# A decoder layer with 32 experts on one core: experts' weights in 1 MB units with 8 KB rows, shift and scale as columns, logits normalized late

## The chip, the core and the metric

The kernel is one launch on one core of a Trainium2 chip. The metric is device time in microseconds (us). TensorE multiplies, VectorE (DVE) and ScalarE (ACT) work on rows of 128 partitions, GpSimd (POOL) does some element work and issues a few DMAs, and SyncE (SP) issues nearly all DMAs, in order. Three runs of the kernel before took 1286.1, 1295.19 and 1295.77 us, with the median at 1295.19.

## The reference

One layer, 256 tokens of width 1024 (`h`), float32. A token mixer (three attention branches, gates, output projection) is followed by a norm, an adaLN modulation by a conditioning vector `c`, a top-4-of-32 mixture of experts with clamped SwiGLU, and a last norm:

```python
x = layer_norm(DN_ALPHA * x + (1.0 + gate) * y, ln1_g, ln1_b)      # y: the mixer's output
shift, scale, gate = split(silu(c) @ mod_ffn_w + mod_ffn_b, 3)
h = x * (1.0 + scale) + shift
logits = h @ router_w + router_b
top_v, top_i = top_k(logits, 4);  combine = one_hot(top_i) * softmax(top_v)
for e in range(32):
    gu = h @ w_gu[e] + b_gu[e]                  # 1024 x 2048
    gate = minimum(gu[:, 0::2], 7.0); up = clip(gu[:, 1::2], -7.0, 7.0)
    act = (up + 1.0) * (gate * sigmoid(1.702 * gate))
    out += combine[:, e:e+1] * (act @ w_down[e] + b_down[e])       # 1024 x 1024
x = layer_norm(DN_ALPHA * x + (1.0 + gate_ffn) * out, ln2_g, ln2_b)
```

Each expert has 12.58 MB of weights, and all 32 have 402.65 MB. Every one is read once.

## The kernel before

**Stages.** By the trace: input projections to about 60 us, keys and values to 100, attention in 24 steps to 222, the branches' products and the output projection to 267, norm and router to 288, the sweep over the experts to 1258, the last norm to 1285.

**Experts.** The experts are sorted by how many tokens chose them, and each is worked on at a *place* with a fixed number of slots: 128 (`Wide`), 64 (`Narrow`) or 32 (`Few`). Four narrow experts come first (0 to 3); then cycles of narrow, wide, few, few. An expert takes 24 steps `t` of half a unit of weights. For a group of places `Group.choose` builds one-hot matrices `sel` on POOL, `Group.gather` brings the tokens' columns into `X` by matmuls with `sel`, `Group.slots` turns `sel` into `selT`, and `Group.weights` gathers the combine weights into `wsl`. Weights are the moving operand of fp32 matmuls (`raw,X` for gate and up, `raw,an` for down; the trace counts two instructions for each fp32 matmul, in two passes). Narrow and few experts split the array in column tiles: a narrow one runs two matmuls side by side, a few one four, so their rows in `y` stand at partitions 0 to 63 and 64 to 127 (or in quarters). A narrow and a few expert are both called split here; there are 25 of them, and 7 wide ones.

**Scatter.** `weigh` (L1288 to L1292) turns an expert's output `y` into two float32r tiles: `yh` on ScalarE, scaled by `wsl`, and the remainder `yl` on VectorE. `leave` then adds both into the four PSUM banks `acc` with `selT` as weights: eight one-pass matmuls, for split experts in pairs of row tiles (`tile_position=(64 n, 0)`), to different banks.

**Loads.** `Stream` hands out weights. `add_units` cuts a unit of 1 MB in two halves, `slot` gives each half a buffer of 512 KB (37 of them, in turn), and one DMA (L148) of 128 rows of 4 KB brings it. In the stages ahead of the experts a unit is one DMA of 1 MB with 8 KB rows, split by `high` (ScalarE) and `low` (VectorE, L165) into `hi` and `lo` tiles of 1024 columns, up to three halves ahead of their use. SP issues in order, a DMA waits for its buffer.

**Conditioning.** `mod_row` makes one row of 1024 of the modulation: `begin` loads a start value into `acc` by an SP DMA, eight `half` tasks multiply and add on VectorE (L687), and `total` sums the partitions by a matmul with ones, two tasks after the last half. There are four rows: gate of layer 2 (`gate2_done`, which sends it to `g2d` by a POOL DMA), gate 1 (`g1h_done`), scale and shift of the experts' norm. `row` (L700) loads two rows to all partitions for the last two.

**Norm and router.** `add` makes the residual `x1` (two operations on VectorE for each of four parts), `spread` its mean and variance, `norm` the normalized `xr` (ScalarE). `turn_norm` transposes it, `logits` multiplies it by `rwg`, `turn_logits` transposes the logits back for the top four. `modulate` makes the experts' input `h2`, two operations of 128x1024 for each half of the tokens. `choose` builds the first group's `sel` on VectorE, and `sort_1` (from L1526) begins the sort of the experts.

TensorE, SP and POOL run in the order of the program; in norm and router VectorE and ScalarE do as well.

Of the kernel before, what the change touches and what calls it, by code (L numbers as in the profile page):

```python
# [16 lines left out]
S = 256  # L17
# [12 lines left out]
RAW_BUFS = 10  # L30
LOW_BUFS = 4
RAW_MORE = 11
PAIRS = 4
AHEAD = 4
# [49 lines left out]
class Stream:  # L84

    def __init__(self, nc, pool, ahead):
        self.nc, self.pool, self.ahead = nc, pool, ahead
        self.todo, self.highs, self.lows, self.parts, self.at = [], 0, 0, {}, {}  # L90
        self.extra, self.big, self.count, self.turn = None, None, 0, True

    def unit(self, ap, m=None):

        n = ap.shape[-1]
        m = m or n // 2
        t = self.pool.tile([128, 2048], F32, tag="raw", name="raw", bufs=RAW_BUFS // 2)
        self.nc.sync.dma_start(out=t[:, :n], in_=ap)
        return t[:, :m], t[:, m:n]

    def slot(self, lasting=False):


        total = RAW_BUFS + 4 + LOW_BUFS + RAW_MORE + 2 * PAIRS if self.turn else RAW_BUFS
        n = self.count % total
        if lasting and (n < RAW_BUFS or n >= total - 2 * PAIRS):
            self.count += RAW_BUFS - n if n < RAW_BUFS else total - n + RAW_BUFS
            n = RAW_BUFS
        self.count += 1
        if n < RAW_BUFS:  # L110
            if n % 2 == 0:
                self.pair = self.pool.tile([128, 2048], F32, tag="raw", name="raw", bufs=RAW_BUFS // 2)
            return self.pair[:, n % 2 * 1024:n % 2 * 1024 + 1024]
        n -= RAW_BUFS
        for pool, tag, bufs in ((self.pool, "hi", 4), (self.pool, "lo", LOW_BUFS), (self.extra, "raw2", RAW_MORE)):
            if n < bufs:
                return pool.tile([128, 1024], F32, tag=tag, name="raw", bufs=bufs)
            n -= bufs
        if n % 2 == 0:
            self.pair = self.big([128, 2048], "raw")  # L120
        return self.pair[:, n % 2 * 1024:n % 2 * 1024 + 1024]

    def low_slot(self):
        return self.pool.tile([128, 1024], F32R, tag="lo", name="lo", bufs=LOW_BUFS)

    def rounded(self):
        return self.pool.tile([128, 1024], F32R, tag="hi", name="hi", bufs=4)

    def add(self, key, get, n=2048, whole=()):

        self.at[key] = len(self.todo)
        self.todo.append((key, get, n, whole))

    def high(self, last):

        while self.highs <= min(last, 2 * len(self.todo) - 1):
            half = self.highs
            u, s = divmod(half, 2)
            key, get, n, whole = self.todo[u]
            m = n // 2  # L140
            if s == 0:
                self.cur = get()
                if not isinstance(self.cur, tuple):
                    self.cur = self.unit(self.cur)
            src = self.cur[s]
            if s in whole:
                src = self.slot()
                self.nc.sync.dma_start(out=src, in_=self.cur[s])  # L148
            self.parts[half] = [src, None, None, m]
            self.highs += 1  # L150
            if s in whole:
                continue
            hi = self.parts[half][1] = self.rounded()
            self.nc.scalar.activation(hi[:, :m], src, AF.Copy)  # L154

    def low(self, last):

        while self.lows <= min(last, self.highs - 1):
            part = self.parts[self.lows]
            src, hi, _, m = part  # L160
            self.lows += 1
            if hi is None:
                continue
            part[2] = self.low_slot()
# [7 lines left out]
    def use(self, key, s):  # L172

        h = 2 * self.at[key] + s
        if self.extra is None:
            self.ensure(h + self.ahead)
        src, hi, lo, m = self.parts.pop(h)
        if hi is None:
            return lambda a, w: src[:, a:a + w]
# [3 lines left out]
def body(tc, A, taps=None):  # L183
# [4 lines left out]
    with ctx:  # L188
# [5 lines left out]
        W = Stream(nc, wp, 3)  # L194
# [19 lines left out]
        def add_units(key, half, slots):  # L214

            def get(v):
                if slots == 128:
                    return half(v, 0), half(v, 1)
                if slots == 64:
                    f, r = divmod(v, 4)  # L220
                    if f < 2:
                        return tuple(half(4 * f + 2 * up + r // 2, r % 2) for up in range(2))
                    return tuple(half(8 + 2 * (r // 2) + n, r % 2) for n in range(2))
                r, pair = divmod(v, 2)
                if r < 4:
                    return tuple(half(4 * pair + 2 * up + r // 2, r % 2) for up in range(2))
                return tuple(half(8 + 2 * f + pair, r - 4) for f in range(2))

            for u in range(12):
                W.add((key, u), lambda u=u: get(u), whole=(0, 1))  # L230

# [13 lines left out]
        def s8(shape, name, dt=F32):  # L245
            return cp.tile(shape, dt, tag="s8", name=name, bufs=6)

        g2d = dp.tile([1, D], F32, name="g2d")
        modd = dp.tile([2, D], F32, name="modd")
        p1 = ExitStack()  # L250
        with p1:
            q = p1.enter_context(tc.tile_pool(name="p1", bufs=1))
# [1561 lines left out]
```

## Time and profile before

| | before |
|---|---|
| median of three runs | 1295.19 us |
| the profiled execution | 1287.11 us, span 1285.3 us |
| TensorE busy | 1184.9 us, 92% |
| VectorE, ScalarE, POOL busy | 417.5, 276.5, 92.2 us |
| DMA | 477.88 MB, 372 GB/s over the span |
| experts' weights | 768 DMAs of 512 KB, 10.1 us each to landing |

The profile is one execution. Busy shares are means over the stages; the slices on the page and windows of the trace tell the stages apart. PEclk is TensorE's granted clock: 1.00 is 2.4 GHz, and the lower level is 1.2 GHz; a value between them is the mean of a window in which both occur.

### The profile page before, as it was taken

Reading aid. Unit: us, or ns where it says so; the run is one execution under the profiler, and the core shown is the slowest. Engines: PE = TensorE matmul, PEld = TensorE weight load, DVE = VectorE, ACT = ScalarE, POOL = GpSimd, SP = SyncE. Lnnn points to the kernel's source line nnn. Section 1 sums busy time; section 2 is a strip of 40 time slices with the busy share of each in tenths; the row PEclk is TensorE's granted clock in tenths of the full one; section 3 lists DMA queues with packets and bytes.
Section 4 is the critical chain, followed back from the end, with each engine's and each line's share of the span. In section 5 each row is a group of like instructions: output and inputs, shape, how many; then the busy total and the mean of one; then the engine's idle time right before and its main releaser. Section 6 shows DMA issues by size and latency. Waiting matters only on the chain. (4 is left out here: it accounts for less than half of the span.)

```text
span 1285.3 us, 17699 instructions
## 1 busy us (share of the span) xinstructions
PE 1184.9 (92%) x6218; PEld 636.5 (50%) x6218; DVE 417.5 (32%) x902; ACT 276.5 (22%) x538; POOL 92.2 (7%) x123
## 2 busy tenths in 40 slices
PE   5989999989999998899799889988998899889982
PEld 5978888974434453344335333433353345334420
DVE  7898888861131121111111111210111112111104
ACT  4555555441111111111111111111011101111112
POOL 0012721000000000000000000000000000000000
PEclk9999999998999999999999989999999999989996
DMA  9987667689999999999999999999999999999992
GB/s 380 355 328 286 255 264 298 216 258 396 406 410 409 407 409 402 409 409 409 409 409 409 408 407 405 408 409 399 408 403 405 402 409 405 406 398 409 395 382 81
DMA packets 125650, 477.88 MB, mean 372 GB/s; under 512 B 15549, under 2 KB 16250, under 8 KB 118896
## 3 DMA queue, kind: packets, MB, share of 16 engines
q1 hardware_dynamic: 123776, 471.36, 93.5%
q0 software_dynamic: 1632, 5.03, 1.2%
q8 instruction: 51, 0.84, 0.3%
q14 instruction: 47, 0.39, 0.1%
q10 hardware_dynamic: 144, 0.26, 0.1%
HBM read 475.52 MB, written 3.44 MB: 373 GB/s over the span
## 5 line engine op out<-in xcount | busy, mean ns | idle before, releaser
L200 PE MATMUL b<-raw,X 128*32 128x512 f32 (+2 forms) x2048 | 479.3, 601 | 0.9 <-DMA raw<-in_wexp 0.9
L200 PE MATMUL b<-raw,an 128*32 128x512 f32 (+2 forms) x1024 | 263.6, 679 | 42.1 <-issue 33.0
L200 PEld LDWEIGHTS b<-raw,X 128*32 128x32 f32 (+2 forms) x2048 | 155.7, 137 | 236.2 <-issue 214.7
L200 PEld LDWEIGHTS b<-raw,an 128*32 128x32 f32 (+2 forms) x1024 | 85.4, 146 | 179.1 <-issue 146.5
L1281 DVE TENSOR_TENSOR gm<-b,biasT 128x256 f32<-128x256 f32 (+1 forms) x50 | 25.0, 499 | 344.3 <-PE b L1297 344.3
L200 PE MATMUL b<-hh,hi 128*128 128x256 f32 x336 | 97.9, 291 | 12.9 <-ACT hh L331 12.9
L1292 DVE SCALAR_TENSOR_TENSOR yl<-b,wsl,yh 128x512 fp32r<-128x512 f32 x39 | 29.3, 750 | 226.7 <-ACT yh L1291 205.9
L1182 POOL TENSOR_SCALAR sel<-cst,pq 128x128 f32<-128x128 f32 x60 | 35.1, 603 | 885.3 <-PE b L200 885.3
L200 PEld LDWEIGHTS b<-sel,h 128*128 128x128 f32 x512 | 76.1, 197 | 43.8 <-issue 42.1
L200 PE MATMUL b<-hh,lo 128*128 128x256 f32 x336 | 95.4, 284 | 1.1 <-DVE lo L165 1.1
L200 PE MATMUL b<-hl,hi 128*128 128x256 f32 x336 | 95.8, 285 | 0.7 <-DVE hl L332 0.7
L200 PE MATMUL b<-sel,h 128*128 128x64 f32 (+2 forms) x512 | 84.0, 310 | 0.1
L165 DVE TENSOR_TENSOR lo<-raw,hi 128x1024 fp32r<-128x1024 f32 (+1 forms) x58 | 70.7, 1234 | 13.5 <-ACT hi L154 10.3
L200 PEld LDWEIGHTS b<-hh,hi 128*128 128x128 f32 x336 | 64.1, 191 | 14.8 <-ACT hh L331 12.9
L1227 ACT ACTIVATE X<-b 128x384 f32<-128x384 f32 (+2 forms) x64 | 24.6, 385 | 200.9 <-PE b L200 200.9
L154 ACT ACTIVATE hi<-raw 128x1024 fp32r<-128x1024 f32 (+1 forms) x58 | 59.5, 1045 | 32.7 <-PE b L200 27.5
L200 PEld LDWEIGHTS b<-hh,lo 128*128 128x128 f32 x336 | 64.3, 191 | 1.6 <-DVE lo L165 1.5
L200 PEld LDWEIGHTS b<-hl,hi 128*128 128x128 f32 x336 | 63.7, 190 | 1.1 <-DVE hl L332 1.1
L1291 ACT ACTIVATE yh<-b,wsl 128x512 fp32r<-128x512 f32 x39 | 26.8, 688 | 160.2 <-PE b L200 160.2
L1297 PEld LDWEIGHTS b<-cst,gu 128*128 128x128 f32 x256 | 29.1, 141 | 56.8 <-issue 32.6
L1297 PE MATMUL b<-cst,gu 128*128 128x128 f32 x256 | 40.4, 280 | 11.5 <-ACT gu L1478 11.5
L1331 ACT ACTIVATE gu<-b 128x512 f32<-128x512 f32 x28 | 16.7, 597 | 128.0 <-PE b L200 128.0
(307 smaller groups left out, 1064.0 us busy)
## 6 DMA issues: line engine op xcount, KB each, us to landing
raw<-in_wexp SPq DMA_DIRECT2D x768, 512.0 KB, 10.1
raw<-in_modg SPq DMA_DIRECT2D x16, 1024.0 KB, 6.4
raw<-in_wmg SPq DMA_DIRECT2D x12, 1024.0 KB, 7.1
raw<-in_moda SPq DMA_DIRECT2D x8, 1024.0 KB, 8.5
raw<-in_wg SPq DMA_DIRECT2D x8, 752.0 KB, 8.1
raw<-in_cw SPq DMA_DIRECT2D x4, 1024.0 KB, 9.1
raw<-in_wbr SPq DMA_DIRECT2D x4, 1024.0 KB, 5.9
raw<-in_wout SPq DMA_DIRECT2D x4, 1024.0 KB, 7.6
```

What stands on the lines that cost most here:

```text
L154: self.nc.scalar.activation(hi[:, :m], src, AF.Copy)
L165: self.nc.vector.tensor_sub(part[2][:, :m], src, hi[:, :m].bitcast(F32))
L200: PE.matmul(out, x, w, start=start, stop=stop, skip_group_check=True, **kw)
L1182: engine.tensor_scalar(out, iota, src[:, i, p:p + 1], None, op0=OP.is_equal)
L1227: at(side, t + 2, lambda: ACT.activation(self.X[:, 2 * c2:2 * c2 + 2, 0:self.width], b[:, 0:2 * self.width].rearrange("p (c w) -> p c w", ...
L1281: V.tensor_tensor(v, z, bias[:, :, None].to_broadcast(shape), OP.add)
L1291: return (yh, yl, lambda: ACT.activation(yh, y, AF.Copy, scale=wsl), lambda: V.scalar_tensor_tensor(yl, y, wsl, yh.bitcast(F32), op0=OP.mu ...
L1292: lambda: V.scalar_tensor_tensor(yl, y, wsl, yh.bitcast(F32), op0=OP.mult, op1=OP.subtract))
L1297: PE.transpose(z[:, j * 128:(j + 1) * 128], gu[:, j * 128:(j + 1) * 128], C("ident"))
L1331: at(side, t, lambda: ACT.activation(gu, b, AF.Copy))
```

## The change

1. **Units.** The experts' weights are laid out anew. A unit of 1 MB is one DMA of 128 rows of 8 KB, and holds the columns of gate and up (or of both halves of down) for two blocks of the contraction. `add_units` no longer cuts it.
2. **Memory.** The pool of the experts' stage (`moe`) is gone. Its tiles, and the units, take buffers of the attention stage as they come free: `FIRST` and `ROUND` list 17 buffers (before 37 halves, 18.5 units). Fourteen units are asked for ahead of the router.
3. **Pairs.** `hi` and `lo` are two double tiles each instead of four single ones, and `W.ahead` is 2 instead of 3.
4. **Columns.** Shift and scale of the experts' norm are made as columns (`mod_column`: 16 operations on VectorE) instead of rows; their two `mod_row`s, 16 of the 32 `half` tasks, and the row loads go. `acc` starts from a POOL memset and a POOL DMA of 4 KB in a tile with a single buffer, and `total` stands in the task of the last half.
5. **Late logits.** The router multiplies the transposed, not normalized `x1` by `rwx`, and the mean and the deviation are put in afterwards. `modulate` is gone: scale `G2` and shift `B2` are put in as the gathered tokens leave PSUM, one half of each pair on ScalarE, one on VectorE.
6. **Scatter.** `weigh` makes one fp32 tile `y` on ScalarE, and the scatter is four fp32 matmuls, eight instructions.

```diff
-RAW_BUFS = 10
-LOW_BUFS = 4
-RAW_MORE = 11
-PAIRS = 4
+RAW = 5
...
-        W = Stream(nc, wp, 3)
+        W = Stream(nc, wp, 2)
...
-            for u in range(12):
-                W.add((key, u), lambda u=u: get(u), whole=(0, 1))
+            for v in ((0, 4, 1, 5, 2, 6, 3, 7, 8, 10, 9, 11) if slots == 32 else range(12)):
+                W.add((key, v), lambda v=v: unit(v), whole=True)
...
+        FIRST = (of(3, lambda: p8("raw", (128, 2048))) + of(2, lambda: s8((128, 2048), "raw"))
+                 + of(RAW, lambda: W.own("raw", RAW)) + of(2, lambda: W.own("hi")) + of(2, lambda: W.own("lo"))
+                 + of(1, lambda: p8("raw", (128, 2048))) + of(1, lambda: s8((128, 2048), "raw")))
+        ROUND = FIRST + of(1, lambda: s8((128, 2048), "raw"))
...
-            def s4(name, shape=(128, D)):
-                return q.tile(list(shape), F32, tag="s4", name=name, bufs=9)
+            def s4(name):
+                return q.tile([128, D], F32, tag="s4", name=name, bufs=1)
...
                     state["a"] = s4("acc")
-                    nc.sync.dma_start(out=state["a"], in_=A["bias0"][bias_row])
+                    POOL.memset(state["a"], 0.0)
+                    POOL.dma_start(out=state["a"][0:1], in_=A["rows"][bias_row:bias_row + 1])
...
+                V.tensor_tensor_reduce(out=state["w"][s], in0=state["w"][s], in1=srow, scale=0.5, scalar=c,
+                                       op0=OP.mult, op1=OP.add, accum_out=c)
...
-                rowtasks[max(8 * a - 4, 0)].insert(0, begin)
-                if 8 * a + 7 + 2 < 32:
-                    rowtasks[8 * a + 7 + 2].append(total)
+                rowtasks[8 * a].insert(0, begin)
+                rowtasks[8 * a + 7].append(total)
...
+            for k in range(8):
+                mm(lgp[:, 64:128], C("ones"), rwx[:, k].rearrange("p n e -> p (n e)"), k == 0, k == 7)
+            outs(3, [(1, 0), (1, 1)])
+            V.tensor_add(rb, rb, lgp[:, 96:128])
             add(0, 0)
...
+                        if c:
+                            V.tensor_scalar(x, v, G2[:, k], B2[:, k], op0=OP.mult, op1=OP.add)
+                        else:
+                            ACT.activation(x, v, AF.Identity, bias=B2[:, k], scale=G2[:, k])
...
-                yh, yl = t2k("yh", 2, F32R), t2k("yl", 1, F32R)
-                return (yh, yl, lambda: ACT.activation(yh, y, AF.Copy, scale=wsl),
-                        lambda: V.scalar_tensor_tensor(yl, y, wsl, yh.bitcast(F32), op0=OP.mult, op1=OP.subtract))
+                z = t2k("y")
+                at(side, t, lambda: ACT.activation(z, y, AF.Copy, scale=self.G.wsl[:, self.slot:self.slot + 1]))
...
-                    for i in range(2):
-                        for yy in (yh, yl):
-                            for n in range(2):
-                                rows = slice(64 * n, 64 * n + 64)
-                                mm(acc[i][n], self.G.selT[rows, self.slot, i * 128:(i + 1) * 128],
-                                   yy[rows], first_of_all(self) and yy is yh, False, tile_position=(64 * n, 0))
+                    for i in range(2):
+                        for n in range(2):
+                            rows = slice(64 * n, 64 * n + 64)
+                            mm(acc[i][n], self.G.selT[self.slot][rows, i * 128:(i + 1) * 128], z[rows],
+                               first_of_all(self), False, tile_position=(64 * n, 0))
```

Three places show how the instructions stand. First TensorE at the scatter of the first expert, before (`h_2988` is the modulated input, `X` the gathered tokens):

```order
L200 MATMUL b<-raw,X 64x512 x4
L200 MATMUL b<-sel,h_2988 128x128 x4
L200 MATMUL b<-yh,selT 128x512 x2
L200 MATMUL b<-yl,selT 128x512 x2
L200 MATMUL b<-yh,selT 128x512 x2
L200 MATMUL b<-yl,selT 128x512 x2
L200 MATMUL b<-raw,X 64x512 x12
```

and after, where units may lie in `hi` and `lo` buffers and `xr` is the normalized, not yet scaled input:

```order
L183 MATMUL b<-raw,an 64x512 x4
L183 MATMUL b<-hi,an 64x512 x8
L183 MATMUL b<-lo,X 64x512 x4
L183 MATMUL b<-sel,xr 128x128 x4
L183 MATMUL b<-y,selT 128x512 x4
L183 MATMUL b<-lo,X 64x512 x4
```

The scatter stands at the same place, between the gather and the next expert's second step; eight float32r matmuls have become four fp32 ones.

Second POOL in the attention steps (`P` are attention maps, `cb` a combined bias), before:

```order
L775 TENSOR_SCALAR P<-P,sm 128x256
L850 TENSOR_TENSOR cb<-bias,work 128x128
L851 TENSOR_TENSOR cb<-bias,work 128x256
L775 TENSOR_SCALAR P<-P,sm 128x128
L775 TENSOR_SCALAR P<-P,sm 128x256
L722 DMA g2d<-g_1598 16x1x64
L850 TENSOR_TENSOR cb<-bias,work 128x128
L851 TENSOR_TENSOR cb<-bias,work 128x256
```

and after:

```order
L753 TENSOR_SCALAR P<-P,sm 128x256
L691 DMA g2d<-cs_81 16x1x64
L828 TENSOR_TENSOR cb<-bias_735,work 128x128
L829 TENSOR_TENSOR cb<-bias_735,work 128x256
L753 TENSOR_SCALAR P<-P,sm 128x128
L753 TENSOR_SCALAR P<-P,sm 128x256
L667 MEMSET acc 128x1024
L668 DMA acc<-in_rows 1x16x64
```

The send of gate 2 now stands ahead of the first combined bias, and the second `acc` is cleared and loaded on POOL, behind that bias and the scaling of a map.

Third VectorE from the end of the output projection on, before (`x_2989` is the residual, `st` its sums):

```order
L165 TENSOR_TENSOR lo<-raw,hi 128x1024
L1012 TENSOR_TENSOR ml<-m,mh 128x512
L1069 TENSOR_TENSOR x_2989<-b,g1h 128x512
L1070 SCALAR_TENSOR_TENSOR x_2989,st_2992<-xr,x_2989 128x512
L1069 TENSOR_TENSOR x_2989<-b,g1h 128x512
```

and after:

```order
L990 TENSOR_TENSOR ml<-m,mh 128x512
L1091 TENSOR_TENSOR rwx<-rw,G_2851 128x8x32
L1091 TENSOR_TENSOR rwx<-rw,B_2852 128x8x32
L1095 TENSOR_TENSOR rb<-rb,b 128x32
L1051 TENSOR_TENSOR x_2875<-b,cs_81 128x512
L1052 SCALAR_TENSOR_TENSOR x_2875,st_2878<-xr,x_2875 128x512
```

The first sum of the residual stands behind `rb`, which reads the product of `rwx` on TensorE; `cs_81` holds gate 1.

## Rows read from the trace of the kernel before

**Rows 1.** The page: its first line, TensorE's busy time, and GB/s in 40 equal slices
```profile
span 1285.3 us, 17699 instructions
...
PE 1184.9 (92%) x6218; PEld 636.5 (50%) x6218; DVE 417.5 (32%) x902; ACT 276.5 (22%) x538; POOL 92.2 (7%) x123
...
GB/s 380 355 328 286 255 264 298 216 258 396 406 410 409 407 409 402 409 409 409 409 409 409 408 407 405 408 409 399 408 403 405 402 409 405 406 398 409 395 382 81
```

**Rows 2.** Two early stretches: us, busy time (instructions) by engine, PEclk, DMA share, GB/s
```profile
10.00:25.00 15.00, 12.14 (x86) 11.92 (x87) 14.12 (x29) 9.26 (x19) 0.85 (x1) 1.00 1.01 422
50.00:65.00 15.00, 14.27 (x123) 12.69 (x122) 11.51 (x29) 9.28 (x18) 0.00 (x0) 1.00 1.01 424
```

**Rows 3.** The same view: four narrow experts, then two cycles of four experts
```profile
412.00:438.20 26.20, 25.57 (x127) 9.12 (x123) 5.30 (x14) 3.31 (x6) 2.33 (x4) 1.00 1.03 408
...
887.70:918.90 31.20, 30.36 (x125) 11.19 (x124) 5.29 (x14) 3.31 (x6) 2.34 (x4) 1.00 1.02 407
1013.00:1043.70 30.70, 29.23 (x128) 11.04 (x124) 5.29 (x14) 3.31 (x6) 2.34 (x4) 1.00 1.02 405
1138.20:1167.60 29.40, 28.55 (x129) 10.52 (x125) 5.29 (x14) 3.31 (x6) 2.33 (x4) 1.00 1.02 409
530.70:648.20 117.50, 109.57 (x542) 48.66 (x538) 20.07 (x43) 15.41 (x29) 4.67 (x8) 0.99 1.03 409
648.20:769.60 121.40, 113.45 (x542) 50.02 (x538) 20.09 (x43) 15.41 (x29) 4.67 (x8) 0.94 1.03 408
```

**Rows 4.** Waits from 880 to 1255 us: us in total, times, longest
```profile
PEld b L200 <- DMA raw<-in_wexp: 20.7, 44, 1.5
...
PE b L200 <- issue: 15.2, 6, 2.5
```

**Rows 5.** TensorE in time order around the scatter of split expert 2: start, us
```profile
382.24 1.89 PE L200 MATMUL b<-raw,X 128*64 128x512 f32 x8
384.05 1.57 PE L200 MATMUL b<-sel,h 128*128 128x192 f32 x8
385.55 0.50 PE L200 MATMUL b<-yh,selT 64*128 64x512 f32 x2
...
386.67 0.65 PE L200 MATMUL b<-raw,X 128*64 128x512 f32 x2
```

**Rows 6.** TensorE in time order, inside wide expert 5 and its scatter
```profile
455.48 1.94 PE L200 MATMUL b<-raw,X 128*128 128x512 f32 x4
457.25 0.60 PE L1297 MATMUL b<-cst,gu 128*128 128x128 f32 x4
...
485.70 0.80 PE L200 MATMUL b<-yh,selT 128*128 128x512 f32 x1
...
488.11 0.50 PE L200 MATMUL b<-yl,selT 128*128 128x512 f32 x1 [0.56 <-DVE yl L1292]
...
489.01 0.64 PE L200 MATMUL b<-raw,X 128*32 128x512 f32 x4
```

**Rows 7.** TensorE in time order, matmuls in four row tiles of 32
```profile
62.61 0.96 PE L200 MATMUL b<-ix 32*128 32x128 f32 x16
```

**Rows 8.** Groups of instructions, 100 to 225 us: busy us, mean ns, idle before
```profile
L687 DVE SCALAR_TENSOR_TENSOR acc<-raw,scol,acc 128x1024 f32<-128x1024 f32 x32 | 42.2, 1320 | 0.3
...
L200 PE MATMUL b<-acc,cst 128*128 128x512 f32 x16 | 7.8, 612 | 0.0
```

**Rows 9.** TensorE's waits, 60 to 290 us
```profile
PE b L200 <- DVE lo L165: 3.3, 3, 2.1
```

**Rows 10.** VectorE in time order, residual sums, top four and sort
```profile
263.43 0.69 DVE L1069 TENSOR_TENSOR x<-b,g1h 128x512 f32<-128x512 f32 x1 [3.86 <-PE b L200]
...
269.75 0.08 DVE L1070 DVE_READ_ACCUMULATOR x<-xr,x 128x1 f32 x1
...
279.71 0.29 DVE L1135 MAX8 v<-b 128x8 f32<-128x32 f32 x2 [2.85 <-PE b L1105]
...
284.13 0.18 DVE L1526 SCALAR_TENSOR_TENSOR key<-cnt,cst 128x32 f32<-128x32 f32 x1
```

More of the change, by code (lines that the diff above doesn't have):

```diff
@@ L89, in __init__, with buffer, own @@
         self.nc, self.pool, self.ahead = nc, pool, ahead
-        self.todo, self.highs, self.lows, self.parts, self.at = [], 0, 0, {}, {}
-        self.extra, self.big, self.count, self.turn = None, None, 0, True
+        self.todo, self.loads, self.highs, self.lows, self.units, self.parts, self.at = [], 0, 0, 0, {}, {}, {}
+        self.others, self.turn = [], 0
+    def buffer(self):
+        if self.others:
+            get = self.others[self.turn]
+            self.turn = (self.turn + 1) % len(self.others)
+            return get()
+        return self.own("raw", RAW)
+    def own(self, tag, bufs=2, dt=F32):
+        return self.pool.tile([128, 2048], dt, tag=tag, name=tag, bufs=bufs)
     def unit(self, ap, m=None):
@@ L96, in unit @@
         m = m or n // 2
-        t = self.pool.tile([128, 2048], F32, tag="raw", name="raw", bufs=RAW_BUFS // 2)
+        t = self.buffer()
         self.nc.sync.dma_start(out=t[:, :n], in_=ap)
         return t[:, :m], t[:, m:n]
[L101 to L129, printed above, removed]
+    def add(self, key, get, n=2048, whole=False):
         self.at[key] = len(self.todo)
         self.todo.append((key, get, n, whole))
+    def load(self, last):
+        while self.loads <= min(last, len(self.todo) - 1):
+            self.units[self.loads] = self.unit(self.todo[self.loads][1]())
+            self.loads += 1
@@ L134, in high @@
     def high(self, last):
         while self.highs <= min(last, 2 * len(self.todo) - 1):
-            half = self.highs
-            u, s = divmod(half, 2)
+            u, s = divmod(self.highs, 2)
             key, get, n, whole = self.todo[u]
+            self.load(u)
             m = n // 2
-            if s == 0:
[L142 to L154, printed above, removed]
+            src = self.units[u][s]
+            part = self.parts[self.highs] = [src, None, None, m]
+            self.highs += 1
+            if whole:
+                continue
+            if s == 0:
+                self.hi = self.own("hi", dt=F32R)
@@ L156, in low @@
+            part[1] = self.hi[:, s * 1024:s * 1024 + 1024]
+            self.nc.scalar.activation(part[1][:, :m], src, AF.Copy)
     def low(self, last):
@@ L1033, in body @@
             merge(1)
[L1034 to L1038 removed]
+            branches(2)
+            rest(2)
+            output(1)
+            merge(2)
+            branches(3)
             rest(len(rowtasks))
[L1041 to L1043 removed]
+            outs(2, [(0, 0), (0, 1), (1, 0)])
+            merge(3)
             xr = s8([128, 2, D], "xr")
@@ L1161, in body, with t2k @@
             V.tensor_copy(cnt, b[:, 64:96])
-        mp = ctx.enter_context(tc.tile_pool(name="moe", bufs=1, reuse_waits="tile"))
-        W.extra, W.big = mp, s8
-        def t2k(name, bufs, dt=F32):
-            return mp.tile([128, 512], dt, tag=name, name=name, bufs=bufs)
-        bgu = W.slot()
-        for e in range(2):
-            nc.sync.dma_start(out=bgu[32 * e:32 * e + 32], in_=A["bgu"][e])
+        W.load(W.at[0, 0] + len(FIRST) - 1)
+        W.others, W.turn = ROUND, 0
+        def t2k(name, dt=F32):
+            return s2(name, (128, 512), dt)
         def choose(sel, src, p, slots, past, engine=POOL):
@@ L1237, in slots, with out @@
                                      self.sel[:, i, s * 128:s * 128 + 128], C("ident"))
-                at(side, t + 2, lambda: ACT.activation(
-                    self.selT[:, 0:n], b[:, 0:n * 256].rearrange("p (s t) -> p s t", s=n), AF.Copy))
+                def out():
+                    for s in range(n):
+                        ACT.activation(self.selT[s], b[:, s * 256:s * 256 + 256], AF.Copy)
+                at(side, t + 2, out)
             def weights(self, t):
@@ L1678, in body @@
                 plan_rows(end - 26 + 6 * n + 2 * m, keep_row, j, n)
-        sweep(experts, end, 2 * W.at[0, 0])
+        sweep(experts, end, W.at[0, 0])
         lng, lnb, g2 = (spread_rows[j] for j in (6, 7, 8))
         more = nc.values_load(order[0:1, 32:33], min_val=0, max_val=1)
-        W.turn = False
+        W.others = []
         with tc.If(more > 0):
```

375 lines of the change are left out of this document (177 added, 198 removed).

## The prediction

> **What bounds the kernel now.** I read the page first. TensorE is busy for 92% of the span, and from the tenth slice on the DMA engines move 395 to 410 GB/s in nearly every slice [rows 1]. Two resources look full at once, so the question is which one sets the pace where. Windows answer it. A narrow expert takes 26.2 us at 412 us, with TensorE busy for 25.6 of them, but 31.2, 30.7 and 29.4 us at 888, 1013 and 1138 us, while the DMA share is 1.02 or 1.03 in all of them [rows 3]. An expert's 12.58 MB at 409 GB/s need 30.8 us, so early narrow experts run ahead of the DMA out of the buffers, and the store is empty from about 880 us on. There the waits name it: TensorE's weight loads wait 20.7 us for the experts' transfers in 44 pieces [rows 4]. Elsewhere a cycle of four experts is TensorE's own: 117.5 us, and 121.4 us for the same work when the granted clock is 0.94 instead of 0.99 [rows 3] (a part of such a cycle runs at the lower of the two levels, 1.2 GHz; TensorE's only long waits there are those of 2.5 us ahead of `an` that the trace names `issue` [rows 4]). So until 880 us, and in wide and most few experts after that, TensorE sets the end; the DMA binds in three late narrow experts. Ahead of 290 us TensorE runs almost without a gap: its largest wait for an operand there is 3.3 us for `lo`, in three pieces [rows 9]. What is added to TensorE's stream is therefore added to the end nearly everywhere.
>
> **Part by part.** The sum is made against the profiled execution, 1287.1 us. It lies 8.1 us (0.6%) under the median of the three runs, 1295.19 us.
>
> *Units of 8 KB rows.* Other loads of the same kernel already have this form. Where they fill the DMA engines, they get 422 and 424 GB/s at share 1.01 [rows 2], against 405 to 409 GB/s with 4 KB rows [rows 3]. All weights, 402.65 MB, then need 950 us in place of 985. A cycle of 50.33 MB needs 118.7 us in place of 123, and TensorE's cycle with the change (below) is about 120.5, so the store of 17 MB never runs dry. What comes back is what the late narrow experts lose, (31.2 + 30.7 + 29.4) - 3 x 26.2 = 12.7 us: -13 us. A bound is 0 (the rate stays at 409), the other -13 and some 3 us in few experts, -16.
>
> The Trainium skill ("DMA: Bandwidth & Descriptors", Rules for kernel authors) asks for 128 partitions and at least 1 MiB in a DMA for the most bandwidth. The rows above agree in direction, though by 4% only; by that rule alone, with the DMA as the bound, the whole stage would follow the transfers, which is rival A.
>
> *More units asked for ahead of the router.* The store is full at the first expert either way, since early narrow experts show no DMA wait: 26.2 us with 25.6 busy [rows 3]. Nothing; if the cover were gone, the loss would be again that of a narrow expert, 5 us each.
>
> *Scatter.* A split expert's scatter now takes from 385.55 to the next matmul at 386.67: 1.12 us for eight one-pass instructions in pairs [rows 5]. The nearest row for four fp32 matmuls, two side by side, is `raw,X` of the same expert: eight instructions from 382.24 to 384.05, 1.81 us [rows 5]. Those pairs are column tiles; the scatter's are row tiles of 64. Row tiles run side by side in fp32 too: 16 instructions of 128 columns in four row tiles are through in 0.96 us [rows 7], where one of 512 columns alone takes (457.25 - 455.48)/4 = 0.44 us [rows 6], so 16 of 128 in a row would take 1.77. So 1.81 us: +0.69 us in each of 25 experts, +17 us. A wide expert's scatter goes from 3.31 us (485.70 to 489.01, of which 0.56 is the wait for `yl`, [rows 6]) to 8 x 0.44 = 3.54 us without that wait: +0.23 in 7, +2 us. Sum +19 us. The lower bound is 0 (the old scatter has a start and an end that the new one may share); the upper is no overlap, 3.54 - 1.12 = 2.42 in 25 experts, +60 us. I take the middle because pairs of the same width are the nearest row. `yl` leaves VectorE, which is not waited for otherwise.
>
> The Trainium skill ("FP8 and Floating Point Precision", TensorE Precision Notes) gives true fp32 four passes, which would double the passes of this scatter (four matmuls of four against eight of one), 1.12 to 2.24 us. Rows show less, 1.81, since a part of the 1.12 is start-up; by the page the term would be an estimated +30 in place of +19.
>
> *Attention steps.* Two `mod_row`s go, and with them two `total`s: eight instructions `acc,cst` of 0.44 us, -3.5 us of TensorE (16 of them stand in the trace [rows 8]; their start to start is taken as that of an fp32 matmul of 512 columns [rows 6]). The 16 `half` tasks of 1.32 us [rows 8] become 16 `mod_column` tasks of one operation of the same size: 0. Against that, `total` now stands right behind the last `half`, so TensorE meets its matmul while VectorE still has that operation of 1.3 us, and what is ahead of it, to do; before there were two tasks between. I take 2.2 us each, +4.5 us (bounds 0 and 3 each, two such operations). The single `acc` makes the second `begin` wait for the first `total`, then for POOL, which holds it behind a bias and a map, then for a DMA; VectorE's eighth task waits some 5 us. TensorE sees of that what its own queue doesn't cover: +2 (0 to 5). `hi` and `lo` as pairs, with two halves ahead: the wait of 3.3 us for `lo` [rows 9] may double: +2 (0 to 4). Together +5, bounds -3.5 and +11.
>
> *Norm and router.* Now: first sum at 263.43, last at 269.75, top four at 279.71, sort from 284.13 [rows 10]. After: `rb` waits for the product of `rwx`, which TensorE reaches three quarters through the output projection, so the first sum starts some 3 us later, and the four sums, 269.75 - 263.43 = 6.3 us, end about 273. But transposes no longer wait for the deviation, two normalizations and two transposes of the logits are off the chain, and `modulate` is gone from VectorE; the top four come 1 us earlier by my count. Then four copies of `X` stand ahead of the sort on VectorE, and the perm matmuls behind it are 1 to 1.5 us later. Net 0, bounds -4 and +4.
>
> *The tail* (the last norm) has the same operations: 0.
>
> Sum: -13 + 19 + 5 + 0 = +11, that is 1298 us: 0.2% over the median. A change under 1% is about what a measurement of this kernel can't tell from none; the marks are 1282.2 and 1308.1 us.
>
> **Rivals.** *A: the transfers set the whole sweep.* DMA share is full throughout [rows 3]. If TensorE's cycle followed it, the sweep would shorten by 985 - 950 = 35 us: 1287 - 35 + 5 = 1257 us. Against it: early narrow experts take 26.2 us where their bytes need 30.8. 0.08.
>
> *B: the fp32 scatter costs nothing* over the old, since the old one too has a start-up and a drain (1.12 us for four pairs). Then 1298 - 19 = 1279 us, faster. For it: the wide expert's row, where eight one-pass instructions and a wait take 3.31 us [rows 6], close to 3.54. Against it: pairs of fp32 at 1.81. 0.17.
>
> *C: row tiles of 64 don't overlap in fp32.* Each pass then stands alone: 3.54 us in split experts, +60 in place of +17: 1341 us, slower. It decides from 2.2 us a split scatter on, which make (2.2 - 1.81) x 25 = 10 us more than the forecast, 1308. For it: no row shows fp32 row tiles of 64. Against it: four row tiles of 32 overlap [rows 7]. 0.12.
>
> *D: the change doesn't do what it says:* 8 KB rows get no more than 409 GB/s in the sweep. Then the 13 us stay lost, but TensorE's extra 19 us fall in part into the late waits: the sweep is the larger of both, 1298 to 1308 us, still within 1%. 0.13.
>
> *E: the attention stage pays its upper bounds* (+11 for +5) and two to three more cycles fall to the lower clock (121.4 against 117.5 us, some 4 us each [rows 3]): 1298 + 6 + 8 to 1298 + 6 + 12, 1312 to 1316 us. 0.1.
>
> **How the numbers follow.** The forecast has 0.4, A 0.08, B 0.17, C 0.12, D 0.13, E 0.1. Faster by over 1%: A and B, 0.25. Slower by over 1%: C and E, and a little of D, 0.25. Within: 0.5. The range leaves A and C out, 0.2: from B with the router's lower bound, 1279 - 7 = 1272 us, to E and a little over, 1318 us. The likeliest case's own range is 1290 to 1307.
>
> **What would show it.** GB/s of 420 or more between 290 and 880 us, or a DMA share under 1 with SP waiting for TensorE, shows the first term; narrow experts of 27 us at 888, 1013 and 1138 us show what it brings. The scatter's start to the next matmul shows the second: 1.8 us, 1.1 (B) or 3.5 (C). For the attention steps: waits of TensorE for `acc`, and VectorE's for the DMA of `acc`; the first expert's first matmul would stand near 293 us, 5 later than now. I am wrong by the sign if TensorE's cycles turn out shorter than 117.5 us, for which no row here gives a reason.

## The result, and the profile after

The changed kernel takes 1301.35 us (median of 17 runs, 1296.2 to 1310.7), the kernel before in the same comparison 1287.92 us (17 runs, 1286.0 to 1295.8). The ratio is 1.0107, with a 95% interval from 1.0086 to 1.0128: slower by 13.4 us. (The median of 1295.19 us that stood ahead of the prediction was high; the profiled execution, 1287.1 us, is the typical one.) The profiled execution of the changed kernel took 1305.3 us.

The page after, first its span, TensorE's busy time and GB/s in 40 equal slices, the lines that answer to [rows 1]:

```profile
span 1303.1 us, 16325 instructions
...
PE 1203.1 (92%) x6208; PEld 638.7 (49%) x6208; DVE 408.6 (31%) x943; ACT 279.0 (21%) x550; POOL 93.0 (7%) x122
...
GB/s 382 345 321 230 237 211 311 265 357 170 384 404 420 421 399 307 420 421 421 412 420 421 420 396 421 421 410 422 421 421 396 421 421 421 385 420 420 409 226 35
```

The transfers are faster, 420 to 422 GB/s where before nearly all slices of the sweep had 395 to 410, and there are now slices of 307, 385 or 396: they no longer fill the sweep. The sweep's narrow experts, windows of the kernel after in the columns of [rows 3]:

```profile
427.30:454.40 27.10, 26.40 (x127) 9.16 (x123) 4.76 (x13) 3.37 (x7) 2.45 (x4) 1.00 1.01 421
911.70:938.80 27.10, 26.40 (x129) 9.20 (x125) 4.76 (x13) 3.37 (x7) 2.45 (x4) 1.00 1.01 420
1034.50:1061.60 27.10, 26.40 (x128) 9.18 (x124) 4.76 (x13) 3.37 (x7) 2.45 (x4) 1.00 1.02 421
1157.40:1184.50 27.10, 26.40 (x129) 9.19 (x125) 4.76 (x13) 3.37 (x7) 2.45 (x4) 1.00 1.01 419
```

Early and late narrow experts take the same 27.1 us; the late ones had taken 31.2, 30.7 and 29.4 [rows 3]. The scatters, TensorE in time order around that of split expert 2 and of wide expert 5, which answer to [rows 5, 6]:

```profile
400.06 1.99 PE L183 MATMUL b<-y,selT 64*128 64x512 f32 x8
401.98 1.51 PE L183 MATMUL b<-raw,X 128*64 128x512 f32 x6
...
503.01 3.60 PE L183 MATMUL b<-y,selT 128*128 128x512 f32 x8
506.54 1.50 PE L183 MATMUL b<-raw,X 128*32 128x512 f32 x12
```

A split scatter takes 1.92 us from start to the next matmul, where it took 1.12, a wide one 3.53, where it took 3.31. TensorE's waits ahead of the sweep (us in total, times, longest), the list that answers to [rows 9]:

```profile
PE b L183 <- DVE lo L147: 3.6, 3, 2.9
PE b L183 <- ACT P L744: 2.1, 1, 2.1
PE b L183 <- DVE acc L674: 1.9, 1, 1.9
PE b L183 <- DVE lg L1064: 1.9, 1, 1.9
PE b L183 <- DVE lg L1108: 1.5, 1, 1.5
PE b L970 <- DVE on L964: 1.2, 1, 1.2
PE b L183 <- DVE ol L974: 0.7, 1, 0.7
PE b L183 <- ACT oh L973: 0.7, 1, 0.7
```

The second and third are the waits of the two row sums (`total`) of the attention steps. The second is named after `P`, but the matmul that it holds up reads `acc`:

```profile
132.54 1.96 PE L183 MATMUL b<-acc,cst 128*128 128x512 f32 x4 [2.09 <-ACT P L744]
```

The last two of the list stand where before a row sum filled the gap in the branches' stage. VectorE in the router, to be read beside [rows 10]:

```profile
275.12 0.19 DVE L1095 TENSOR_TENSOR rb<-rb,b 128x32 f32<-128x32 f32 x1 [5.18 <-PE b L183]
275.23 0.68 DVE L1051 TENSOR_TENSOR x<-b,cs 128x512 f32<-128x512 f32 x1
...
290.97 0.31 DVE L1120 MAX8 v<-lg 128x8 f32<-128x32 f32 x2
...
301.45 0.18 DVE L1508 SCALAR_TENSOR_TENSOR key<-cnt,cst 128x32 f32<-128x32 f32 x1
```

Read by stage, the two profiled executions differ by 14.6 us at the first expert's first matmul (303.0 against 288.4 us) and by 3.9 us in the sweep (979.1 against 975.2 us to the end of its last weight matmul, which before is at 1263.6 us and not at the 1258 of the list of stages). The 14.6 are +1.3 up to the attention steps, +4.7 in them, +4.3 in branches and output projection, +2.3 from there to the first gather, +2.0 from the gather to the first expert. The 14.6 is more than is usual: three other executions with the same work ahead of the sweep have 8.1 (E1), 10.2 (E2) and 10.3 us (E10).

### The profile page after: what moved, and what is told of

Read it like the earlier page. It is cut to its first block, busy times and chain, and to the rows that moved or that the text cites. A ratio compares the mean times of both kernels' runs of the same rounds, so it can differ in the third digit from the quotient of the medians.

```text
span 1303.1 us, 16325 instructions
## 1 busy us (share of the span) xinstructions
PE 1203.1 (92%) x6208; PEld 638.7 (49%) x6208; DVE 408.6 (31%) x943; ACT 279.0 (21%) x550; POOL 93.0 (7%) x122
## 5 line engine op out<-in xcount | busy, mean ns | idle before, releaser
L183 PE MATMUL b<-raw,X 128*32 128x512 f32 (+2 forms) x1584 | 362.4, 599 | 0.0
L183 PE MATMUL b<-raw,an 128*32 128x512 f32 (+2 forms) x776 | 203.6, 675 | 26.1 <-DVE an L1369 15.9
L183 PEld LDWEIGHTS b<-raw,X 128*32 128x32 f32 (+2 forms) x1584 | 116.5, 136 | 188.7 <-issue 182.8
L1214 DVE TENSOR_SCALAR X<-b,G,B 128x192 f32<-128x192 f32 (+2 forms) x64 | 26.3, 410 | 400.5 <-ACT X L1216 400.5
L183 PEld LDWEIGHTS b<-sel,xr 128*128 128x128 f32 x512 | 75.8, 197 | 43.7 <-issue 42.1
L1216 ACT ACTIVATE X<-b,B,G 128x192 f32<-128x192 f32 (+2 forms) x64 | 29.3, 457 | 258.2 <-PE b L183 258.2
L183 PE MATMUL b<-sel,xr 128*128 128x64 f32 (+2 forms) x512 | 83.6, 309 | 0.1
L183 PE MATMUL b<-y,selT 64*128 64x512 f32 (+1 forms) x256 | 74.9, 610 | 0.9 <-ACT y L1282 0.9
L183 PE MATMUL b<-lo,X 128*32 128x512 f32 (+2 forms) x232 | 64.7, 598 | 0.0
L183 PE MATMUL b<-hi,X 128*32 128x512 f32 (+2 forms) x232 | 63.2, 598 | 0.0
## 6 DMA issues: line engine op xcount, KB each, us to landing
lo<-in_wexp SPq DMA_DIRECT2D x44, 1024.0 KB, 14.5
```

The lines of the kernel that those rows point to most:

```text
L183: PE.matmul(out, x, w, start=start, stop=stop, skip_group_check=True, **kw)
L1214: V.tensor_scalar(x, v, G2[:, k], B2[:, k], op0=OP.mult, op1=OP.add)
L1216: ACT.activation(x, v, AF.Identity, bias=B2[:, k], scale=G2[:, k])
```

## The experiments

Each was timed beside the kernel before, which took 1287.1 us (E1 to E4), 1288.6 us (E5 to E8) and 1287.5 us (E9 to E11). A ratio is that of the run to the kernel before, with its 95% interval.

**E1, 4 KB rows in the changed kernel.** Only the experts' DMAs are cut in two:

```diff
-        self.nc.sync.dma_start(out=t[:, :n], in_=ap)
+        self.nc.sync.dma_start(out=t[:, :m], in_=ap[:, :m])
+        self.nc.sync.dma_start(out=t[:, m:n], in_=ap[:, m:n])
```

> The changed kernel with each unit of the experts' weights fetched as two DMAs of 512 KB with 4 KB rows, as before; buffers and everything else as changed. Theory (TensorE sets the sweep, since the slower scatter made its cycle of four experts about 122 us, and the transfers need 123 us at 409 GB/s): the rate falls from 421 to about 409 GB/s, and the time rises by 0 to 4 us only, 1301 to 1305 us. Rival (the 8 KB rows bring back the 12.7 us of the late narrow experts in any case): 1313 to 1317 us, narrow experts of 29 us and more from 900 us on.

1299.8 us, ratio 1.0125 (1.0089 to 1.0160). The changed kernel's interval holds it. Windows of its narrow experts at 905 and 1151 us:

```profile
905.20:932.20 27.00, 26.30 (x128) 9.14 (x124) 4.76 (x13) 3.37 (x7) 2.45 (x4) 1.00 1.03 407
1150.90:1178.80 27.90, 27.31 (x128) 9.79 (x124) 4.75 (x13) 3.37 (x7) 2.44 (x4) 1.00 1.02 402
```

At 407 GB/s only the last narrow expert waits, 0.9 us. In this kernel the 8 KB rows bring nothing that can be measured. (Here and in E8 the length of a row and the size of a DMA change together, so the runs don't tell which of the two gives the rate.)

**E2, the old scatter in the changed kernel.** `yh` and `yl` in float32r and eight one-pass matmuls:

```diff
-                z = t2k("y")
-                at(side, t, lambda: ACT.activation(z, y, AF.Copy, scale=self.G.wsl[:, self.slot:self.slot + 1]))
+                yh, yl = t2k("yh", F32R), t2k("yl", F32R)
+                at(side, t, lambda: ACT.activation(yh, y, AF.Copy, scale=wsl))
+                at(side, t + 1, lambda: V.scalar_tensor_tensor(yl, y, wsl, yh.bitcast(F32), op0=OP.mult, op1=OP.subtract))
```

> The changed kernel with the scatter of before (yh and yl, eight one-pass matmuls). Theory (the scatter costs 25 x 0.77 + 7 x 0.23 = 20.8 us of TensorE, and all of it is on the path): split scatters back to 1.15 us, wide ones to 3.3; 1301 - 21 = 1280 us, ratio to before about 0.995, with narrow experts of 26.3 us. Rival 1 (the transfers bind as soon as TensorE is faster): 1288 to 1293 us, with late narrow experts of 28 us and more. Rival 2 (what the sweep lost lies elsewhere): above 1293 us.

1284.1 us, ratio 0.9983 (0.9966 to 0.9999): 17 us less than the changed kernel. The time lies between the 1280 of the theory and the 1288 of the first rival. Split scatters are back at 1.13 us, wide ones at 3.03 (under the 3.31 of before), the narrow experts from the fifth on at 26.3, as early ones were before, and the sweep at 962.3 us, 16.8 us shorter than the changed kernel's and 12.9 shorter than before's. Without the new scatter the loss is gone.

**E3, dummy matmuls ahead of the sweep.** Eight in the branches' stage, eight behind either transposition in the router:

```diff
                 rest(len(rowtasks))
+                warm(8)
                 branch_half(0, 1)
...
             turn_sum(0)
+            warm(8, lgp[:, 128:256])
```

> The changed kernel with eight dummy matmuls at each of three places where TensorE waits (ahead of the second half of the first branch product, and after either transposition of the residual in the router). Theory (short waits there let TensorE's clock fall to 1.2 GHz for 7 us in the branches and some 12 us in the router, which costs 3 and 4 us): granted clock near 1.00 in both stretches, 1301 - 7 = 1294 us. Rival (only the waits themselves cost, the clock would have fallen anyway or doesn't matter): 1300 to 1304 us, since the dummies fill waits or add to them.

1302.2 us, ratio 1.0109 (1.0078 to 1.0140): no gain, as the rival had it. In its profile the clock does stay up in the router, where the changed kernel's had fallen to the lower level (in the branches it is 0.83 from 226 to 236 us, so not all was filled there). The first two lines are windows of the kernel after, the third of E3:

```profile
228.00:236.80 8.80, 7.39 (x33) 6.61 (x34) 6.07 (x10) 2.82 (x4) 0.00 (x0) 0.61 0.32 126
281.00:286.00 5.00, 4.65 (x23) 4.25 (x22) 2.08 (x6) 3.77 (x6) 0.00 (x0) 0.52 1.02 429
```

```profile
280.00:290.00 10.00, 8.94 (x76) 8.40 (x75) 5.97 (x29) 5.10 (x9) 0.00 (x0) 1.00 0.89 371
```

and the first expert begins at 295.9 us instead of 303.0. But its sweep is 10.7 us longer: 7.4 in the few experts (307.5 us in sum instead of 300.1), 3.3 in the narrow ones, nearly all in the second, where the clock is 0.91 instead of 1.00. The place where the clock falls varies from one execution to the next, and one profile of either kernel is no measure of it. Nor was it the dummies that brought the first expert forward: from the end of the output projection to the first gather E3 takes 14.9 us, and so do E1, E2 and E10 without any.

**E4, the new scatter in the kernel before.**

```diff
-                yh, yl = t2k("yh", 2, F32R), t2k("yl", 1, F32R)
+                yh = t2k("yh", 2)                # plain fp32; selT fp32 too, no yl
```

> The kernel before with the fp32 scatter alone (one fp32 tile y, four fp32 matmuls). Theory (TensorE gets 20.8 us more, but about 13 us of it falls into the waits for weights that the late narrow experts had anyway at 409 GB/s): 1288 + 8 = 1296 us, 1294 to 1300, ratio 1.005 to 1.009. Rival (the extra is paid in full, as the DMA never really bound): 1309 us, ratio 1.016.

1291.9 us, ratio 1.0033 (1.0020 to 1.0047): +4.8 us, less than expected. The same scatter that costs 17 us in the changed kernel costs 5 here. Its narrow experts at 901 and 1144 us:

```profile
901.00:928.10 27.10, 26.47 (x129) 9.22 (x125) 4.55 (x13) 3.31 (x6) 2.33 (x4) 1.00 1.02 404
1143.50:1172.20 28.70, 28.19 (x129) 10.48 (x125) 4.55 (x13) 3.31 (x6) 2.33 (x4) 1.00 1.03 410
```

The waits for weights of [rows 3] are gone at 404 GB/s but for 1.6 us in the last narrow expert, because TensorE is now slow enough for it. Its sweep, 979.8 us, is that of the changed kernel, 979.1.

**E5, the modulation's tasks in another order.** Row of gate 2, 16 columns, row of gate 1; sums two tasks later:

```diff
-                rowtasks[8 * a].insert(0, begin)
-                rowtasks[8 * a + 7].append(total)
+            rowtasks[0].insert(0, rows[0][0])
+            rowtasks[9].append(rows[0][2])
+            rowtasks[14].append(rows[1][0])
+            rowtasks.append([rows[1][2]])
```

> The changed kernel with the modulation's tasks in another order: the row of gate 2, then the 16 columns, then the row of gate 1; a row's sum (total) two tasks after its last half, as before, so that the last one falls into the branches' stage; the second start value of acc long ahead of its use. Theory (the sum right behind the last half costs TensorE 2.2 and 2.1 us of waiting, and without a sum in the branches' stage TensorE idles 1.9 us for oh and ol and its clock falls there): 1301 - 4 - 2 = 1295 us, up to 4 us less where clock falls go with the waits; no wait for acc, last branch product 5 us earlier. Rival (VectorE is late by the same amount anyway, the waits come back at the next reader): 1299 to 1303 us.

1299.9 us, ratio 1.0069 (1.0030 to 1.0108). That is in the rival's range (1299 to 1303), and the 1295 of the theory was not reached. In its profile the waits for `P`, `acc`, `ol` and `oh` are gone, the last matmul of the branch products begins at 253.4 us instead of 264.6, and the first expert at 287.9, 8.6 to 10.9 us ahead of E1, E2 and E10. But the sweep of this execution takes 988.8 us, 9.7 more than the changed kernel's, at a lower clock in the first two narrow experts (0.89 and 0.95 for 0.94 and 1.00) and in the few (306.4 us in sum for 300.1). The waits that went are shown; a gain in the time is not.

**E6, two moves in the router.**

```diff
-            V.tensor_add(rb, rb, lgp[:, 96:128])
             add(0, 0)
...
             turn_sum(0)
+            V.tensor_add(rb, rb, lgp[:, 96:128])
             factors(0)
...
         G0.choose(V)
+        sort_1()
```

> The changed kernel with two moves in the router: the sum into rb stands behind the residual's sums, just ahead of its first reader, and the first step of the sort stands right behind the choice, ahead of the four copies of X. Theory: the first residual sum no longer waits 5.2 us for the product of rwx, and the last one ends 2 to 3 us earlier; the perm matmuls no longer wait 1.9 us; first expert 4 to 5 us earlier, 1301 - 4.5 = 1296.5 us. Rival (the last residual sum waits for the end of the output projection anyway, and the sort's copies only move behind): 0 to -2 us, 1299 to 1301 us.

1304.8 us, ratio 1.0105 (1.0062 to 1.0148). The time shows no gain; it is even over the rival's range, though the ratio is that of the changed kernel. Of the two moves one works. TensorE no longer waits for `perm`, and from the first gather to the first expert it takes 4.3 us instead of 6.3, as before the change. The first residual sum begins at 268.9 us, ahead of the output projection's last matmul at 275.8, but the last sum still waits for the end of that projection, and from there to the first gather it takes 14.9 us as without the move. The few experts of this execution ran at the lower clock more (307.3 us in sum). Below 2 us of gain this comparison can't tell.

**E7, the parts together:** the old scatter (E2), the tasks' order (E5), the router's order (E6) and the router's dummies (E3).

> The changed kernel with the old float32r scatter, the tasks' order of e5, the router's order of e6 and dummy matmuls in two waits of the router. Theory (the parts add up: 1284 - 5 - 4.5): 1275 us, 1271 to 1279, ratio to before 0.990; narrow experts 26.3 us throughout. Rival (the transfers bind once the sweep begins earlier, and give half of it back): 1279 to 1284 us, with narrow experts of 27 us and more after 1000 us.

1275.0 us (1274.0 to 1276.1), ratio 0.9886 (0.9851 to 0.9922). Faster than both kernels, where the theory put it. The parts don't add up everywhere: from the end of the output projection to the first gather E7 takes 17.0 us, where E3, E5 and E6 take 14.9 each. Why is open.

**E8, the same with 4 KB rows** (the edit of E1).

> As e7, with the experts' units fetched as two DMAs of 512 KB with 4 KB rows. Theory (with the fast scatter TensorE's cycle is about 118 us, under the 123 us that 409 GB/s need, so here the 8 KB rows are worth what the late narrow experts lose): 8 to 13 us more than e7, 1283 to 1288 us, late narrow experts of 29 us and more. Rival (8 KB rows bring nothing, the other changes of buffers and loads did): within 2 us of e7.

1289.4 us, ratio 1.0002 (0.9980 to 1.0023): 14 us more than E7, just over the 8 to 13 expected. Here the 8 KB rows are worth what the prediction gave them. A late narrow expert of E7, then of E8:

```profile
1009.30:1035.60 26.30, 25.60 (x128) 9.16 (x124) 5.51 (x14) 3.37 (x7) 2.45 (x4) 1.00 1.01 421
```

```profile
1013.60:1044.20 30.60, 29.67 (x125) 11.12 (x124) 5.51 (x14) 3.37 (x7) 2.44 (x4) 1.00 1.02 408
```

**E9 to E11, the wait of the few experts filled.** A few expert makes TensorE wait 2.5 us for `an` [rows 4]. Nine dummy matmuls go there, in E7 (E9), in the changed kernel (E10) and in the kernel before (E11):

```diff
                 def turned():
                     self.act[0] = self.activation(
...
+                    for _ in range(9):
+                        mm(b[:, 0:128], C("ident"), C("ident"), True, True)
```

> As e7, with nine dummy matmuls of 128 columns (some 2.3 us) in each few expert, between the transposition of its gate and up and the matmuls that wait 2.5 us for an. Theory (that wait is what makes TensorE's clock fall to 1.2 GHz for 3 to 6 us behind it, and TensorE sets the sweep): granted clock over 0.98, few experts near 18 to 19.5 us instead of 21.4, 14 x 2 to 3 us less, until the transfers (956 us at 421 GB/s) set the end: 1275 - 20 to 35, 1240 to 1255 us. Rival (the clock falls for another reason, or the dummies lie on the path): 1272 us or more.

> The changed kernel with the same nine dummies in each few expert and nothing else. Theory (its spread from 1296 to 1311 us is how often and how long the clock falls in the few experts, paid in full since TensorE sets the sweep): 1301 - 20 to 30, 1271 to 1281 us, and the runs lie within 5 us of one another. Rival (the spread has another cause): runs still 10 us apart and more, 1296 us or over.

> The kernel before with the same nine dummies in each few expert. Theory (before, the transfers set the end of the sweep at 409 GB/s, so a TensorE that gains 20 to 30 us only reaches the empty store earlier and waits longer for weights): 1288 - 0 to 5, 1283 to 1288 us, late narrow experts of 31 us from an earlier one on. Rival (TensorE set the end before as well): 1268 us or less.

E9: 1261.1 us, ratio 0.9791 (0.9769 to 0.9812). E10: 1280.5 us (1276.8 to 1284.3), ratio 0.9949 (0.9931 to 0.9968), 21 us less than the changed kernel; its runs lie 7.5 us apart, not within the 5 expected; the changed kernel's lie 14.5 apart. E11: 1286.6 us, ratio 0.9990 (0.9974 to 1.0005), no difference. Two pairs of few experts, first of the changed kernel, then of E10:

```profile
626.80:669.40 42.60, 36.01 (x253) 14.53 (x252) 6.46 (x17) 5.41 (x11) 0.00 (x0) 0.92 1.00 413
1113.80:1157.40 43.60, 37.01 (x253) 14.98 (x252) 6.46 (x17) 5.41 (x11) 0.00 (x0) 0.88 0.96 398
```

```profile
620.90:660.20 39.30, 36.73 (x289) 17.62 (x288) 6.46 (x17) 5.42 (x11) 0.00 (x0) 1.00 1.01 420
1095.30:1134.70 39.40, 36.83 (x291) 17.65 (x290) 6.46 (x17) 5.42 (x11) 0.00 (x0) 1.00 1.01 421
```

With the wait filled the granted clock stays at 1.00, and a pair takes 39.3 to 39.4 us instead of 42.6 and 43.6. All few experts together take 275.6 us instead of 300.1, and the changed kernel gets nearly all of that back. The kernel before gets nothing: its TensorE only reaches the empty store earlier. E11's narrow experts:

```profile
762.60:794.00 31.40, 29.83 (x125) 11.29 (x124) 5.30 (x14) 3.31 (x6) 2.34 (x4) 1.00 1.02 407
887.30:918.60 31.30, 30.78 (x125) 11.02 (x124) 5.30 (x14) 3.31 (x6) 2.35 (x4) 1.00 1.02 401
```

The narrow expert at 763 us, which took 26.2 us in the kernel before, already waits for weights. In E9, where TensorE is fastest, the transfers bind again at 8 KB rows:

```profile
759.60:786.10 26.50, 25.70 (x129) 9.21 (x125) 5.51 (x14) 3.44 (x8) 2.45 (x4) 1.00 1.01 421
875.70:905.60 29.90, 26.76 (x125) 8.91 (x125) 5.51 (x14) 3.60 (x8) 2.45 (x4) 1.00 1.01 423
```

which is why it gained 14 us, not the 20 to 35 expected.

## Why the prediction was right, and where it was not

**The number and the direction.** 1298 us was forecast, 11 us over the profiled execution; it was 1301.35, 13.4 over the median. The range held it. It was forecast to lie within 1%, and the ratio, 1.0107, lies just outside, with an interval over both sides of that mark.

**What bounds the kernel before.** This step failed, though the sum came out. The prediction took TensorE for the bound until 880 us and in most of the rest, since TensorE ran without a wait there. But a wait that appears only at the end is where an account over the whole sweep is settled. The experts' loads begin at 236 us, and 402.65 MB at 405 to 409 GB/s need 985 to 994 us, more than the whole sweep of 975. What SP, which issues the loads, waits for from 290 to 1255 us (us in total, times, longest) shows the two kernels apart. Before:

```profile
SPq L148 <- DMA raw<-in_wexp: 527.2, 703, 1.6
SPq L148 <- PE b L200: 21.8, 62, 4.0
```

and after:

```profile
SPq L105 <- PE b L183: 466.0, 198, 22.9
SPq L105 <- DMA raw<-in_wexp: 202.5, 114, 2.0
```

Before, SP waits for earlier DMAs and hardly ever (21.8 us) for TensorE to free a buffer, so the transfers run through the sweep without a pause, and a store of 18.5 units only shifts when TensorE notices. In the changed kernel the transfers wait 466.0 us for TensorE. So the prediction's "the store is full at the first expert either way" failed with it: that TensorE doesn't wait says nothing of a full store. E11 shows the same in time: its first four few experts take 77.5 us instead of 82.1, then TensorE meets the waits earlier, nothing is gained, and the last expert starts at 1239.4 us against 1241.4. E8's last one starts at 1240.9. The row that said so was read and set aside: a DMA share of 1.02 in every window of [rows 3]. Rival A ("the transfers set the whole sweep") was right about the kernel before; its price was wrong, since with the change the bound passes to TensorE.

**8 KB rows, -13 us.** The rate is as forecast (421 GB/s against 424), and the size is right where the transfers bind: 14 us between E7 and E8. In the changed kernel they bring nothing (E1), because the slower scatter lets 409 GB/s suffice. The Trainium skill's rule of at least 1 MiB in a DMA ("DMA: Bandwidth & Descriptors", Rules for kernel authors) agrees with E7 and E8, by the same 14 us; with E1 it makes no difference.

**The scatter, +19 us.** The size on TensorE was nearly right: 1.92 us for 1.81 forecast, 3.53 for 3.54, thus 25 x 0.79 + 7 x 0.22 = 21 us by rows (median of the split scatters 1.13 us before, 1.92 after). Row tiles of 64 do overlap in fp32, so rival C fell, and rival B as well. What was wrong is that terms were added that are not independent: in the kernel before this costs 4.8 us (E4), in the changed one 17 (E2). -13 and +19 were each measured against a different bound. Their sum, +6, fits the sweep (+3.9) since E4's +4.8 and E1's 0 add up to nearly the same; that the sum came out is luck. The prediction's own rival D named that interplay and put it at 0.13. The Trainium skill's four passes for true fp32 ("FP8 and Floating Point Precision", TensorE Precision Notes) would have made an estimated 2.24 us of a split scatter; the rows show 1.92.

**Attention, +5 us.** The sum was right, +4.7 in the profile, its parts only in half. Windows of the attention steps, before, after, and in E1:

```profile
112.28:214.73 102.45, 102.45 (x732) 90.20 (x731) 87.97 (x184) 52.72 (x127) 43.93 (x43) 1.00 0.70 263
113.57:220.73 107.16, 102.71 (x728) 90.62 (x727) 85.49 (x196) 52.47 (x127) 43.98 (x42) 0.98 0.66 244
113.69:218.58 104.89, 100.87 (x728) 89.45 (x727) 85.81 (x196) 52.48 (x127) 43.70 (x42) 1.00 0.67 250
```

The two sums that stay cost waits of 2.1 and 1.9 us for 2.2 each. But of the 3.5 us that two sums less were to bring, only one sum's 1.6 is here (102.45 to 100.87 us in E1, four instructions less); the other had stood in the branches' stage. And TensorE idles 4.45 us in all, so the two terms of +2, for `acc` on POOL and for `lo`, are not there (`lo` 3.6 us for 3.3). In their place come 1.8 us of the clock, 0.98 for 1.00 (102.71 us busy where E1 has 100.87). With the clock up, as in E1, the stage costs 2.4 us and not 5, so this sum was luck in part.

**Branches, norm and router, 0 us.** The prediction has no term for the branches' stage, and that was the miss: branches and output projection take 57.2 us for 52.9, +4.3, and 56.1 to 56.8 in E1, E2 and E10. In E5, which puts a row sum back into that stage, 54.7 are left; the 1.8 over before fit the product of `rwx`, 1.7 us from 273.19 to 274.89 in TensorE's stream between two parts of the output projection. Without that sum TensorE saves its 1.9 us, but waits 1.4 us for `oh` and `ol` and has a clock of 0.61 from 228.0 to 236.8 us: 1.5 to 2.5 us more in all. The router's own term of 0 was right in its net, and the +4.3 there in the profile are an exception. From the end of the output projection to the first gather before, after, and in E10:

```profile
267.59:284.16 16.57, 13.09 (x100) 10.80 (x101) 11.30 (x39) 9.26 (x18) 0.00 (x0) 0.90 0.83 283
277.93:296.79 18.86, 15.32 (x83) 14.54 (x81) 9.66 (x42) 8.40 (x14) 0.00 (x0) 0.64 0.69 278
277.64:292.54 14.90, 11.20 (x83) 10.59 (x81) 9.57 (x42) 8.41 (x14) 0.00 (x0) 0.89 0.87 352
```

At a clock of 0.64 the same matmuls keep TensorE busy for 15.3 us instead of 11.2. At 0.89 this stretch takes 1.7 us less than before, and the same 14.9 us in E1, E2, E3, E5 and E6. So the gain of 1 us forecast is there, and the sort behind the copies of `X` takes it back, 2.0 us where 1 to 1.5 were forecast.

**The range.** Its lower end takes 7 us for "the router's lower bound"; the prediction's own bound is 4, and the other 3 fit only the -16 of its first term. Nothing hangs on it here.

**The clock.** Case E spoke of it as a tail; it is a main term of the changed kernel. Its runs follow their mean granted clock: 1296.2 us at 0.970, 1301.4 at 0.965, 1310.7 at 0.955, about 0.9 us for each 0.001. The kernel before, over the 41 runs beside E1 to E8, between 0.958 and 0.975, follows its clock loosely, by 0.3 us for each 0.001 (0.05 in one comparison, 0.5 in the other). So a fall costs more where TensorE sets the end. It is not free where the transfers do: E8's 11 runs move by 0.6 us for each 0.001. E10 confirms the clock's part in the changed kernel by taking the falls in the few experts away.

Left open: why the clock falls in one execution and not in another at the same place. The 14.6 us ahead of the sweep are high for that reason; E1, E2 and E10 give 8.1 to 10.3.

## What to carry to other kernels

When a deep store of buffers stands between a full transfer queue and a full engine, look at what the issuer of the loads waits for over the whole stage: if it hardly waits for a free buffer (here 21.8 us before and 466.0 after, and 56.8 in E1, where the two are nearly even), the transfers are the bound, even where the engine hardly waits. Don't add a gain in transfers to a loss in compute as if both counted: only the larger of the two paths does, and an edit's worth (here 0 or 14 us for the same 8 KB rows, 5 or 17 for the same scatter) depends on which one that is. And when an edit makes TensorE the bound, look for waits of a few us that bring its clock down, and fill them: nine dummy matmuls in 14 experts gave back more than the whole change had cost.

## What the runs showed of the hardware

- Two row tiles of 64 in fp32, to different banks, overlap: eight instructions of 512 columns take 1.92 us in pairs, and eight over all 128 rows 3.53 us one by one.
- DMAs of 1 MB with 8 KB rows moved 421 GB/s in the sweep, DMAs of 512 KB with 4 KB rows 402 to 410, at a DMA share of 1.01 to 1.03 in both; size and row length changed together.
- Behind TensorE's waits of 2.5 us in few experts the granted clock of a pair was 0.88 to 0.92; with dummies in that wait it was 1.00, and the pair took 3 to 4 us less (39.3 and 39.4 for 42.6 and 43.6).
